# Layer B's attention: one copy per output bank, halves turned by DMA and added by GpSimd, and narrower second-dilation products

## The chip, the cores and the metric

The kernel runs on one core of one Trainium2 chip, as a single program. A time is the device time of one execution in microseconds (us); three executions of the kernel before took 3033.78, 3033.9 and 3038.08 us, median 3033.9. The core has five engines that each run their own list of instructions in order and wait for one another through semaphores: TensorE (PE; its weight loads are shown as PEld), VectorE (DVE), ScalarE (ACT), GpSimd (POOL) and SyncE (SP). SP computes nothing here: it issues DMA transfers, one after the other, and waits before an issue if the transfer's source isn't ready or its target is still in use. TensorE writes to PSUM banks of 128 partitions by 512 float32; DVE and ACT read them.

## The reference

A two-layer decoder trunk on 1024 tokens of width 1024: layer A with native sparse attention and a SwiGLU block, then layer B, whose queries attend over shared keys and values in three head groups of different dilation, and a second SwiGLU block. Only layer B's attention is touched:

```
DILATIONS = ((128, 1), (512, 4), (2048, 16))       # (window, dilation)
def banded_attention(q, k, v, max_dist, dist_scale, rel_bias):
    s = einsum(q, k) * dh ** -0.5                  # per block of 128 queries
    p, denom, m = masked_softmax(s + bias, mask)   # unnormalised exp, its sum, row max
    o = einsum(p, v) / denom
    lse = log(denom) + m
def dilated_attention(h, w_q, k_shared, v_shared, w_out, rel_bias):
    ...                                            # the three (o, lse), merged by softmax over lse
    return o @ w_out
```

There are 16 heads in 4 groups of 4 (g = 0..3), each of 64 columns, and 8 blocks of 128 queries. Dilations 4 and 16 are both handled on tokens ordered by residue modulo 8: a block r of 128 queries of one residue needs 256 keys for dilation 4 and 128 for dilation 16.

## The kernel before, in words

**Precision.** float32 values are used in TensorE as a pair of `float32r` tiles, high and low (`split`, L132: ACT copies the rounded high part, DVE subtracts it). For keys and queries the pair lies in one tile of 128 partitions, high in 64, low in 64.

**Work of a unit.** For each group there are 8 *wide* units (`wide_job`, r = 0..7: dilations 4 and 16 together, 384 columns of scores) and then 8 *near* units (`near_job`, t = 0..7: dilation 1, 128 or 256 columns). Each unit is two jobs, `hp` = 0 and 1, of two heads `e` each. The front of a job (`unit`) makes the score products on PE, adds the bias and takes the row extreme on DVE (L1453), and exponentiates on ACT (L1458). The back, two jobs later (`pipelined(jobs(), 2)`), transposes the probabilities on PE (`transposed`, L275), brings them to SBUF as a pair (`th`, `tl`, L138 and L139), and multiplies by the values into a bank `o` (`mm_pv`, L296 to L298). Banks: 3 for scores (`s`), 3 for transposes (`pt`), 2 for outputs (`o`).

- In a wide unit, one value block is *late*: only the last 64 queries of it count. Its transpose is copied raw, by ACT for hp 0 and DVE for hp 1 (L289), and split by POOL (L290, L291); with `bufs` 5 these share `th` and `tl` with the rest.
- In a near unit, hp 1 isn't split: its transpose is copied raw (L281), by ACT for even t and DVE for odd t, and multiplied as plain float32 (L296).
- The score product of dilation 16 (L1494) is 256 columns wide, of which the last 128 are never read; the last r has 128.

**Evacuation.** Products of values' high and low halves stand in the two partition halves of the bank and are to be added across them. When hp 1 is done, `evac_o` (L302) does this for e = 0, 1: ACT copies the 64 partitions of the other half to SBUF (`ot`, L308), and DVE adds the bank's own half to it (L309), into `o12` (wide) or `oT` (near). `evac_o` is also layer A's.

**Merging and loads.** `merge(g)` weights the two outputs (rows L1524 to L1572), partly among group g's near jobs, partly among group g + 1's wide jobs. Queries, keys, values and bias tables of a group are loaded by SP from HBM into rings of fixed slots: `load` (L1415 queries, L267 and L268 keys, L1419 values), `load_T12` (L1426, L1427) and `load_T0` (L1435, whose tables POOL then masks, L1436). A load waits until the slot's last reader is done. A group's loads are about 13 MB, 11 MB of it in 27 transfers of 256 or 512 KB. SP's transfers use eight semaphores in turn, so transfer n is issued only when transfer n - 8 has landed.

**Order.** The lists of all engines, SP's and POOL's too, are set at build time by a scheduler that plays the program through with its own estimates of time; on the chip each engine runs its list as it stands.

## Time and profile before

The profiled execution spans 3035.7 us on the core (granted clock 0.983 on the mean); the median of the timed executions is 1.8 us below that span.

| stretch of the trace, us | what | length | PE busy | DVE busy | ACT busy | POOL busy | DMA share |
|---|---|---|---|---|---|---|---|
| 0 to 1925 | layer A, its SwiGLU, projections for B | 1925.0 | 1855.8 | 1452.8 | 1004.7 | 1095.5 | 0.35 |
| 1925 to 2245.5 | layer B's attention | 320.5 | 293.82 | 274.28 | 278.60 | 95.50 | 0.60 |
| 2245.5 to 3035.7 | output projection, SwiGLU, final norm | 790.2 | 749.65 | 674.61 | 320.23 | 439.07 | 0.18 |

Busy time is time in which an engine works, by its instructions' spans; spans of neighbouring instructions overlap a little, so an engine can be full below 100%. "DMA share" is the mean busy share of the 16 DMA engines. An instruction's group has a row with its line, engine, operation, names (out<-in), shape, count, then busy us and mean ns of one, then the idle time of the engine before it and what ended that.

### The profile page before, as it was taken

How to read it: one execution, taken by the hardware profiler on the slowest of the kernel's cores; microseconds unless marked ns; L12 is line 12 of the kernel's file. 1: busy time of each engine (PE TensorE's matmuls, PEld its weight loads, DVE VectorE, ACT ScalarE, POOL GpSimd, SP SyncE). 2: the span in 40 equal slices, each digit the busy share in tenths (PEclk: the TensorE clock that was granted, in tenths of full speed). 3: DMA queues.
4: the chain of work that ended last, by engine and by line, in shares of the span. 5: the costliest groups of instructions: out<-in, count | busy, mean ns of one | idle time of the engine just before them, and what ended most of it. 6: DMA issues, size and time to landing. Idle time of an engine off the chain costs nothing.

```text
span 3035.7 us, 44147 instructions
## 1 busy us (share of the span) xinstructions
PE 2899.3 (96%) x14670; PEld 2381.4 (78%) x14670; DVE 2401.7 (79%) x4832; ACT 1603.6 (53%) x3596; POOL 1630.1 (54%) x1751
## 2 busy tenths in 40 slices
PE   7999999999889999999999999899988899999997
PEld 6987888888677877777777778788866787777776
DVE  4432888988988888888876677589899788888887
ACT  5432888887463333333364444689965433333334
POOL 2134666666766555555556787333357755555551
PEclk9999999999999999999999999999999999999999
DMA  6765032121112222222124555876420211112111
GB/s 167 223 191 165 25 103 78 36 56 70 60 53 63 63 67 74 65 59 70 56 95 141 160 160 145 264 209 179 138 94 25 66 55 57 56 46 62 51 45 73
DMA packets 266196, 293.43 MB, mean 97 GB/s; under 512 B 17971, under 2 KB 209347, under 8 KB 265968
## 3 DMA queue, kind: packets, MB, share of 16 engines
q1 hardware_dynamic: 246320, 230.45, 26.3%
q0 software_dynamic: 19648, 60.16, 6.6%
q8 instruction: 116, 1.90, 0.3%
q14 instruction: 112, 0.92, 0.1%
HBM read 227.44 MB, written 78.81 MB: 101 GB/s over the span
## 4 chain that ended last, share of the span: by engine, by line
PE 68%; DVE 16%; ACT 5%; issue 4%; DMA 4%; POOL 2%; SPq 1%; DVEq 0%; ACTq 0%; POOLq 0%
PE ux L165 5%; PE ux L166 5%; PE ux L167 5%; PE uy L166 4%; PE uy L165 4%; PE uy L167 4%; DVE pl L762 4%; PE pt L275 4%; PE dx L166 3%; PE dr L165 3%; PE dx L167 3%; PE dx L165 3%; PE dr L166 3%; PE dr L167 3%; PE mm L165 3%
## 5 line engine op out<-in xcount | busy, mean ns | idle before, releaser
L762 DVE TENSOR_TENSOR pl<-oT,ph 128x512 fp32r<-128x512 f32 x315 | 325.2, 1052 | 41.3 <-ACT ph L761 35.4
L761 ACT ACTIVATE ph<-oT 128x512 fp32r<-128x512 f32 x329 | 199.0, 626 | 228.1 <-PE ux L166 65.8
L275 PE MATMUL pt<-ident,P 128*128 128x128 f32 x1536 | 245.1, 278 | 11.0 <-ACT P L1458 2.7
L761 ACT ACTIVATE ph<-oTb 128x512 fp32r<-128x512 f32 x239 | 143.2, 625 | 189.4 <-PE ux L166 55.7
L762 DVE TENSOR_TENSOR pl<-oTb,ph 128x512 fp32r<-128x512 f32 x229 | 224.4, 1005 | 23.5 <-ACT ph L761 23.4
L820 DVE TENSOR_TENSOR xr<-xr,dr 128x512 f32<-128x512 f32 x336 | 214.6, 679 | 33.9 <-PE dr L167 33.8
L139 DVE TENSOR_TENSOR tl<-pt,th 128x512 fp32r<-128x512 f32 (+1 forms) x320 | 207.1, 651 | 33.8 <-ACT th L138 31.9
L820 DVE TENSOR_TENSOR xr<-xr,dx 128x512 f32<-128x512 f32 x352 | 220.3, 678 | 3.6 <-PE dx L167 2.4
L166 PE MATMUL dx<-pl,ph 128*128 128x512 f32 x512 | 203.4, 401 | 9.7 <-DVE pl L762 9.0
L688 POOL TENSOR_SCALAR P<-P,sm,gates 128x384 f32<-128x384 f32 (+7 forms) x256 | 183.5, 728 | 53.4 <-DVE sm L686 48.0
L275 PEld LDWEIGHTS pt<-ident,P 128*128 128x128 f32 x1536 | 179.8, 142 | 30.0 <-ACT P L1458 6.7
L138 ACT ACTIVATE th<-pt 128x512 fp32r<-128x512 f32 (+1 forms) x320 | 177.2, 563 | 44.3 <-PE pt L275 40.4
L167 PE MATMUL dx<-ph,pl 128*128 128x512 f32 x512 | 200.0, 397 | 0.3 <-DVE pl L762 0.3
L684 ACT ACTIVATE P<-P,m 128x384 f32<-128x384 f32 (+7 forms) x256 | 170.7, 669 | 16.1 <-DVE m L682 8.4
L1081 POOL TENSOR_TENSOR oT<-oT,gffn 128x512 f32<-128x512 f32 x92 | 105.9, 1158 | 136.2 <-DMA oT<-in_ffn_w_up_dram 110.5
L165 PE MATMUL dx<-ph 128*128 128x512 f32 x512 | 157.3, 400 | 6.7 <-DVE xr L820 3.3
L1081 POOL TENSOR_TENSOR oTb<-oTb,gffn 128x512 f32<-128x512 f32 x92 | 106.4, 1165 | 99.1 <-DMA oTb<-in_ffn_w_up_dram 77.0
L298 PE MATMUL o<-tl,V 128*128 128x256 f32 x540 | 148.8, 299 | 7.4 <-POOL tl L291 3.7
L297 PE MATMUL o<-th,V 128*128 128x256 f32 x540 | 151.4, 296 | 2.7 <-ACT th L138 1.4
L290 POOL TENSOR_SCALAR th<-traw 128x128 fp32r<-128x128 f32 (+1 forms) x112 | 75.1, 674 | 129.3 <-ACT traw L289 47.7
L1458 ACT ACTIVATE P<-P,st 128x384 f32<-128x384 f32 (+2 forms) x256 | 139.6, 547 | 7.6 <-PE pt L1569 4.1
L166 PEld LDWEIGHTS dx<-pl,ph 128*128 128x128 f32 x512 | 97.6, 191 | 39.5 <-DVE pl L762 19.4
(617 smaller groups left out, 9582.4 us busy)
## 6 DMA issues: line engine op xcount, KB each, us to landing
qB<-xr POOLq DMA_DIRECT2D x96, 256.0 KB, 4.7
oT<-in_ffn_w_up_dram SPq DMA_DIRECT2D x92, 256.0 KB, 3.0
oTb<-in_ffn_w_up_dram SPq DMA_DIRECT2D x92, 256.0 KB, 3.0
Q<-qB SPq DMA_DIRECT2D x40, 512.0 KB, 7.0
wd<-in_ffn_w_down_dram SPq DMA_DIRECT2D x66, 256.0 KB, 2.6
oT<-in_b_w_q_dram SPq DMA_DIRECT2D x48, 256.0 KB, 3.5
K<-kBs SPq DMA_DIRECT2D x40, 256.0 KB, 9.5
wraw<-in_a_w_in_dram SPq DMA_DIRECT2D x18, 512.0 KB, 4.9
```

Source lines behind the costliest of these rows:

```text
L138: nc.scalar.activation(H_, src, AF.Copy)
L139: nc.vector.tensor_sub(L_, src, f32(H_))
L165: nc.tensor.matmul(ps, lh, rh, start=first, stop=False, skip_group_check=bool(shared))
L166: nc.tensor.matmul(ps, lh, rl, start=False, stop=False, skip_group_check=bool(shared))
L167: return nc.tensor.matmul(ps, ll, rh, start=False, stop=last, skip_group_check=bool(shared))
L275: nc.tensor.transpose(ps[:, i * 128:(i + 1) * 128], b, ident)
L684: nc.scalar.activation(P[:, e, :n], P[:, e, :n], AF.Exp, bias=mm[:, e:e + 1], scale=-1.0, accum_out=sm[:, e:e + 1])
L688: nc.gpsimd.tensor_scalar(P[:, e, :n], P[:, e, :n], sm[:, e:e + 1], gt(g, t, br, 2 * hp + e, 1), op0=OP.mult, op1=OP.mult)
L761: nc.scalar.activation(h, src, AF.Copy)
L762: (eng or nc.vector).tensor_sub(l, src, f32(h))
L820: nc.vector.tensor_add(xs, xs, banks[t])
L1081: nc.gpsimd.tensor_mul(v, v, gains[:, k:k + 4].unsqueeze(2).to_broadcast([128, 4, 128]))
```

## The change

- **Evacuation.** A new `evac_shifted` takes the place of `evac_o` in layer B. The whole bank is copied once to SBUF (`oraw`, two buffers), by ACT for even units and by DVE for odd ones. Then, for each half, SP issues a DMA that moves the other half's 64 partitions by 256 columns (64 KB) across the partitions (`oturn`, two buffers), and POOL adds the two in SBUF. The bank is free after the copy.
- **Second dilation's product.** 128 columns instead of 256, for all r. The first loads of its keys take equal pieces instead of overlapping by 128 columns.
- **Copies.** The late copies and the raw copies of near units are all made by DVE.
- **Buffers.** Late blocks get tiles of their own (`thq`, `tlq`, 128 columns, two buffers); `th` and `tl` have 4 buffers instead of 5; `T0`'s ring has 4 slots instead of 5.

```diff
@@ transposed
-        th = p.tile([128, 512], F32R, name="th", bufs=bufs)
-        tl = p.tile([128, 512], F32R, name="tl", bufs=bufs)
+        z = [128, 128] if q0 else [128, 512]
+        th, tl = [p.tile(z, F32R, name=n + "q" * (q0 > 0), bufs=2 if q0 else bufs) for n in ("th", "tl")]
@@ rings
-        rT0 = Ring("T0", [128, 256], F32, [(bB, 5)])
+        rT0 = Ring("T0", [128, 256], F32, [(bB, 4)])
@@ load_first
-                    ks = slice(2 * lo, 2 * hi) if i == 1 else slice(lo + 128 * (lo > 0), min(hi + 128, S))
+                    ks = slice(2 * lo, 2 * hi) if i == 1 else slice(lo, hi)
@@ before unit
-        unsplit = lambda key, hp: (cp_a, cp_v)[key[2] % 2] if key[1] == 0 and hp == 1 else None
+        def evac_shifted(po, dst, copy):
+
+            ov = po[:].rearrange("p (c e q) -> p e c q", e=2, q=128)
+            raw = wk.tile([128, 2, 2, 128], F32, name="oraw", bufs=2)
+            turn = wk.tile([128, 2, 128], F32, name="oturn", bufs=2)
+            copy(raw, ov)
+            for e in range(2):
+                own, oth = slice(64 * e, 64 * e + 64), slice(64 - 64 * e, 128 - 64 * e)
+                nc.sync.dma_start(turn[own], raw[oth, e])
+                nc.gpsimd.tensor_add(dst[own], raw[own, e], turn[own])
+
+        unsplit = lambda key, hp: cp_v if key[1] == 0 and hp == 1 else None
@@ unit, back
-                th, tl = transposed(wk, of(bs), None, 5, unsplit(key, hp))
+                th, tl = transposed(wk, of(bs), None, 4, unsplit(key, hp))
...
-                    th, tl = transposed(wk, of([late]), (cp_a, cp_v)[hp], 5, q0=64)
+                    th, tl = transposed(wk, of([late]), cp_v, 5, q0=64)
...
-                    evac_o(wk, po, dst)
+                    evac_shifted(po, dst, (cp_a, cp_v)[key[2] % 2])
@@ wide_job, score
-                w = min(256, S - r * 128)
                 with after(prev):
                     for z in range(2):
-                        nc.tensor.matmul(ps[:, 256:256 + w], Q2[hh][:, qs], K2[z][:, r * 128:r * 128 + w],
-                                         start=z == 0, stop=z == 1)
+                        nc.tensor.matmul(ps[:, 256:384], Q2[hh][:, qs], K2[z][:, qs], start=z == 0, stop=z == 1)
```

The scheduler makes new lists from it. Two places matter below.

**SP, where group 0 hands over to group 1** (the loads of group 1's second-dilation tiles: K is its keys, Q its queries, T the bias tables). Before:

```order
L267 DMA K_20381<-kBs 64x1024
L268 DMA K_20381<-kBs 64x1024
L267 DMA K_20382<-kBs 64x1024
L268 DMA K_20382<-kBs 64x1024
L1415 DMA Q_20378<-qB 128x1024
L1415 DMA Q_20379<-qB 128x1024
L1415 DMA Q_20380<-qB 128x1024
L1426 DMA T_20393<-s_76 128x256
L1427 DMA T_20393<-s_77 128x128
L1426 DMA T_20396<-s_76 128x256
L1427 DMA T_20396<-s_77 128x128
```

And now:

```order
L267 DMA K_20399<-kBs 64x1024
L268 DMA K_20399<-kBs 64x1024
L267 DMA K_20400<-kBs 64x1024
L268 DMA K_20400<-kBs 64x1024
L1415 DMA Q_20396<-qB 128x1024
L1415 DMA Q_20397<-qB 128x1024
L1415 DMA Q_20398<-qB 128x1024
L1426 DMA T_20411<-s_76 128x256
L1427 DMA T_20411<-s_77 128x128
L1426 DMA T_20414<-s_76 128x256
L1427 DMA T_20414<-s_77 128x128
L1451 DMA oturn<-oraw 64x256 x4
```

The loads stand as before, but the four turning transfers of group 0's wide units r = 5 and 6 now stand behind them, in the same list. Of the same kind: the four of r = 1 and 2 stand ahead of group 1's first load; then 12 loads come, then the four of r = 3 and 4, then 16 loads (the end of which is shown), then these.

**POOL, where group 1 hands over to group 2** (`th`, `tl` the late blocks' pair, T the first dilation's bias tables). Before:

```order
L290 TENSOR_SCALAR th<-traw 128x128
L291 TENSOR_TENSOR tl<-traw,th 128x128
L1436 AFFINE_SELECT T_22190<-T_22190 128x256
L1436 AFFINE_SELECT T_22195<-T_22195 128x256
L1436 AFFINE_SELECT T_22200<-T_22200 128x256
L1436 AFFINE_SELECT T_23435<-T_23435 128x256
L290 TENSOR_SCALAR th<-traw 128x128
```

And now:

```order
L1452 TENSOR_TENSOR o_20773<-oraw,oturn 64x2x128 x6
L1452 TENSOR_TENSOR oTb<-oraw,oturn 64x2x128 x14
L1436 AFFINE_SELECT T_22251<-T_22251 128x256
L1436 AFFINE_SELECT T_22256<-T_22256 128x256
L1436 AFFINE_SELECT T_22261<-T_22261 128x256
L290 TENSOR_SCALAR thq<-traw 128x128
L1436 AFFINE_SELECT T_22266<-T_22266 128x256
L291 TENSOR_TENSOR tlq<-traw,thq 128x128
L1452 TENSOR_TENSOR oTb<-oraw,oturn 64x2x128 x2
```

POOL had nothing between the last late block of a group and the masking of the tables; now the additions of the last three wide and of seven near units stand there, and the eighth near unit's stand behind the masking.

## The prediction

> **What bounds the kernel now.** I read the spans first, then the busy times by stretch, cut at the first score product of each wide and near stage of layer B's attention (wide, near, of groups 0 to 3 in turn; the columns are PE, PEld, DVE, ACT, POOL, clock, DMA share, GB/s).
>
> ```profile
> core 0: 3035.7 us, clock 0.983
> ...
> 1925.30:1965.20 39.90, 34.65 (x271) 34.00 (x269) 27.79 (x87) 32.24 (x90) 13.21 (x27) 0.91 0.91 275
> 1965.20:1998.00 32.80, 28.04 (x206) 25.50 (x205) 26.06 (x103) 29.05 (x91) 6.75 (x15) 0.95 1.01 275
> 1998.00:2043.50 45.50, 43.90 (x331) 39.86 (x329) 41.53 (x125) 38.96 (x114) 19.12 (x32) 1.00 0.52 153
> 2043.50:2075.40 31.90, 29.50 (x228) 26.53 (x226) 27.76 (x106) 31.25 (x98) 5.01 (x11) 1.00 0.92 252
> 2075.40:2118.80 43.40, 41.73 (x320) 38.14 (x319) 39.90 (x122) 36.88 (x106) 18.18 (x30) 1.00 0.41 129
> 2118.80:2149.10 30.30, 28.04 (x216) 24.76 (x214) 26.52 (x106) 29.67 (x95) 4.65 (x10) 1.00 0.90 249
> 2149.10:2193.90 44.80, 42.86 (x326) 39.28 (x325) 40.38 (x121) 38.08 (x110) 18.29 (x30) 1.00 0.29 85
> 2193.90:2224.50 30.60, 26.10 (x199) 23.03 (x199) 27.92 (x107) 30.04 (x93) 4.58 (x10) 1.00 0.33 124
> ```
>
> A wide stage takes some 44.5 us and is PE's (96% busy) with DVE close behind (91%). A near stage takes some 31 us and is ACT's (98%), DVE at 88%. POOL is idle three quarters of the time. The first two stretches are different: the DMA engines are full, because group 0's and group 1's loads run back to back. In near stages of groups 1 and 2 they are full again (0.92, 0.90) with the next group's loads. So what I ask of the change is what it takes from PE and DVE in wide stages, from ACT and DVE in near ones, and what its transfers meet in SP's queue.
>
> **What it takes from the engines.** Groups by form, over the attention alone:
>
> ```profile
> L308 ACT ACTIVATE ot<-o 64x256 f32<-64x256 f32 x128 | 48.5, 379 | 14.9 <-PE o L296 4.6 <-DVE oTb L309 4.0 <-PE o L298 2.7
> L309 DVE TENSOR_TENSOR oTb<-o,ot 64x256 f32<-64x256 f32 x64 | 26.9, 421 | 8.4 <-ACT ot L308 7.1
> L309 DVE TENSOR_TENSOR o<-o,ot 64x256 f32<-64x256 f32 x64 | 26.9, 420 | 5.8 <-ACT ot L308 4.3
> L281 DVE COPY traw<-pt 128x512 f32<-128x512 f32 x16 | 10.9, 684 | 3.1 <-issue 3.0
> L281 ACT COPY traw<-pt 128x512 f32<-128x512 f32 x12 | 7.0, 581 | 0.2
> L281 ACT COPY traw<-pt 128x256 f32<-128x256 f32 x4 | 1.4, 357 | 0.0
> L289 DVE COPY traw<-pt 128x128 f32<-128x128 f32 x32 | 9.1, 285 | 3.4 <-POOL tl L291 1.1 <-PE pt L275 0.8 <-POOL th L290 0.6
> L289 ACT COPY traw<-pt 128x128 f32<-128x128 f32 x32 | 8.2, 257 | 3.6 <-PE pt L275 3.5
> L1494 PE MATMUL s<-K,Q 128*128 128x256 f32 x224 | 44.9, 285 | 0.0
> L1494 PE MATMUL s<-K,Q 128*128 128x128 f32 x32 | 5.4, 249 | 0.0
> ```
>
> ACT loses 48.5 + 8.2 + 7.0 + 1.4 = 65.1 us and gains 32 whole-bank copies, priced as its own 512-column copy of a bank, 0.581: 18.6. Net -46.5, or -11.6 a group. DVE loses 53.8 and gains 32 copies by 0.684 (21.9), 32 late copies by 0.285 (9.1) and ACT's 16 near copies (12 by 0.684 and 4 of 256 columns by 0.42, between the rows of 128 and 512: 9.9). Net -12.9, or -3.2 a group.
>
> PE: 224 products become half as wide. The rows above give 44.9/224 = 0.200 us and 5.4/32 = 0.169, a saving of 0.031 each. In a stretch where nothing waits, starts lie 0.12 apart at 256 columns and 0.06 after one of 128:
>
> ```profile
> 2111.01 0.28 PE L297 MATMUL o<-th,V 128*128 128x256 f32 x1
> 2111.13 0.28 PE L298 MATMUL o<-tl,V 128*128 128x256 f32 x1
> 2111.25 0.23 PE L297 MATMUL o<-th,V 128*128 128x128 f32 x1
> 2111.31 0.29 PE L275 MATMUL pt<-ident,P 128*128 128x128 f32 x1
> ```
>
> So 224 by 0.031 to 0.06, 7 to 13.4 us, all in wide stages: 1.7 to 3.4 a group.
>
> On the path less counts. In wide stages DVE loses 16 additions (6.7) and gains 4 bank copies (2.7) and 8 late ones (2.3): -1.7; it stands 3 us behind PE. In near stages ACT loses 16 copies of 0.379 and its near copies (2.1) and gains 4 bank copies (2.3): -5.9; DVE, 3.5 behind ACT, loses 6.7 and gains 2.7 and 2.5: -1.5. If the busiest engine alone set each stage, a wide one would shrink by 3.4 and a near one by 3.5 + 1.5 = 5.0, together 8.4 a group and 34 in all. But every job passes through DVE, which works 88 to 91% of both stages, and gives up only 1.5 to 1.7 in each. I take 1.5 for each stage: -3 a group, **-12** in all (bounds 0 and -34). The smaller rings (`T0`, `th`, `tl`) and the first keys' cut I take as nothing: late blocks leave `th` and `tl`, and the first key loads only change their cut.
>
> **What it adds.** POOL gets 128 additions of 64x256. The trace has none with 64 partitions; nearest are POOL's subtraction at 256 columns in layer A and, as upper bound, the strided addition of 512:
>
> ```profile
> L291 POOL TENSOR_TENSOR tl<-traw,th 128x256 fp32r<-128x256 f32 x48 | 35.3, 736 | 0.8
> L1572 POOL TENSOR_TENSOR oTb<-oTb,o 128x512 f32<-128x512 f32 x12 | 19.2, 1618 | 2.6 <-DVE o L1570 2.6
> ```
>
> I take 0.74, the same size: 23.7 us a group on top of POOL's 23, of 75. Hidden.
>
> SP gets 128 transfers of 64 KB. Landing times from issue, in group 0's near stage and, after it, in a quiet stretch of group 2's wide stage:
>
> ```profile
> Q<-qB SPq DMA_DIRECT2D x10, 512.0 KB, 9.5
> K<-kBs SPq DMA_DIRECT2D x9, 256.0 KB, 10.3
> ...
> T<-s SPq DMA_DIRECT2D x4, 128.0 KB, 2.3
> T<-s SPq DMA_DIRECT2D x4, 64.0 KB, 2.1
> ```
>
> and, in a full stretch, SP's issues follow landings (a load can only go when the eighth before it is in):
>
> ```profile
> 2046.52 0.45 SPq L268 DMA_DIRECT2D K<-kBs  x1
> 2047.82 0.33 SPq L1415 DMA_DIRECT2D Q<-qB  x1
> 2049.14 0.44 SPq L267 DMA_DIRECT2D K<-kBs  x1
> 2050.81 0.45 SPq L268 DMA_DIRECT2D K<-kBs  x1
> ```
>
> So a turn takes 2.1 us when the queue is quiet and about 10 when it is full. `oraw` and `oturn` have two buffers, so in a lap of copy (0.7), turn, and two additions (1.5) two units can be evacuated. Quiet: 4.3 us for two, against 9.4 that two units take (75/16 each). Full: 12.2 for two, 6.1 a unit, against 3.9 in a near stage.
>
> First hand-over, group 0 to 1. In SP's new list, turns of units r = 3, 4 stand behind 12 loads and those of r = 5, 6 behind 16 more. At 1.0 to 1.7 us a load (the four rows above) and two buffers plus two `o` banks ahead of the turns, four units can be in flight; the next product with values waits on PE, and everything behind it. A block of 16 loads of mixed size takes some 16 us; in it two units come free, worth 2 x 3.9. So some 8 us are lost behind each of two blocks: +16. From below: if the loads have mostly landed by then, only the turns' own bytes count in a stretch that is full anyway, 32 x 64 KB at 275 GB/s = 7.6. From above, full laps for all 8 near units and 3 wide ones: 11 x 2.2 = 24.
>
> Groups 1 and 2: near stages are full for about two thirds, five units; 5 x 2.2 = 11 as an upper bound each. There the list has only two to four loads between turns, so the queue never fills as before; I take +2 each (0 to 11). Group 3 loads nothing, so 0. At the end the last addition comes a turn and a POOL addition later than ACT and DVE's: 2.1 + 1.5 - 0.8, +3.
>
> Sum: -12 + 16 + 4 + 3 = +11, on 3035.7: 3046.7 in its own profile. The median stood 1.8 below the span: **3045**.
>
> **The rivals.**
>
> *The queue doesn't bind (3025).* Turns land in 2.1 us, if turns and loads interleave on the chip; then only -12 and +3 are left: -9 on 3033.9 is 3025. For it: the attention's DMA share is 0.60 on the mean, and ACT's 98% is real. Against it: landings of 10 us in the stretch where these turns stand. The Trainium skill, page "DMA: Bandwidth & Descriptors", section "Anatomy of one DMA — SWDGE (gpsimd) path", fits a transfer as 2.0 us plus its bytes over 436 GB/s; for a turn an estimate of 2.15 us by that page. The quiet rows agree (2.1), the full ones don't (9.5 to 10.3). Chance 0.19.
>
> *Gain and loss cancel (3034).* The first hand-over costs its lower bound, 7.6, the rest nothing: -12 + 7.6 + 3 = -1. Chance 0.16.
>
> *Every full near stage throttles (3060).* Groups 1 and 2 pay 10 each and group 0 the same 16: -12 + 16 + 20 + 3 = +27. For it: the windows' 0.92 and 0.90. Against it: near loads there may wait, nobody needs them for 20 us. It decides from the third near unit on, at `copy(raw, ov)`, which sits in ACT's and DVE's lists ahead of the next exponentials. Chance 0.2.
>
> *POOL becomes the bound (3080 and more).* At the strided price, 1.6 us, POOL has 23 + 51 = 74 us a group, and its list makes it wait for tables besides:
>
> ```profile
> POOL T L1436 <- DMA T<-sA: 80.5, 6, 24.0
> ```
>
> Some 15 more a group, three times: +45. The strides of the new additions are whole runs of 128, unlike that row's, so 0.03.
>
> *The narrow product doesn't save.* If it costs what 256 columns cost, 6 us come back: inside the range.
>
> **How the numbers follow.** Chances: forecast 0.42, then 0.19, 0.16, 0.2 and 0.03. About 0.2%, 6 us, is what a measurement of this kernel can tell from no change: faster is under 3027.8, slower over 3040.0. The forecast and the two slow rivals are slower: 0.65; cancelling is the same: 0.16; the first rival is faster: 0.19. The range for 8 in 10, from just over the first rival's time to just over the third's: 3026 to 3062; the forecast's own is 3040 to 3053 (first hand-over 11 to 19, gain -15 to -9, ends rounded).
>
> **What would show it.** In the profile after: POOL's L1452 at about 0.74 us; L1451's landing near 2 us in wide stages of groups 1 to 3 and near 10 between 1965 and 2000; ACT's busy time in the attention down by some 46 us, DVE's by some 13; the first score product of group 1 (now at 1998.0) about 13 us later, with long waits on `oturn` at L1452 and on the copies; later groups 72 to 76 us each, as against 73.7 to 77.4. If group 1 starts on time, the forecast is wrong in its main term, and 3026 to 3034 is what is left. If L1452 takes 1.5 us, or groups 1 and 2 take over 80 us each, it is too low.

## The result, and the profile after

The changed kernel takes 3083.9 us (median of 4, 3079.65 to 3089.1), the one before 3036.0 in the same runs: a ratio of 1.0148, 95% interval 1.013 to 1.0167 (the ratio of the two medians, which differs a little, is 1.0158). By the medians that is 48 us slower, against a forecast of 11. Its profiled execution spans 3087.3 us, 51.6 more than that of before.

The windows of the changed kernel, cut as in the prediction (near stage of group 0, then wide and near of groups 1 and 2, wide of group 3; columns PE, PEld, DVE, ACT, POOL, clock, DMA share, GB/s):

```profile
1965.80:1996.50 30.70, 26.09 (x183) 22.16 (x180) 22.39 (x91) 22.79 (x75) 11.74 (x22) 0.94 0.98 278
1996.50:2065.30 68.80, 54.20 (x364) 47.60 (x362) 43.11 (x124) 34.31 (x96) 39.04 (x59) 0.90 0.55 155
2065.30:2103.00 37.70, 29.16 (x222) 26.26 (x220) 26.30 (x100) 25.28 (x82) 13.69 (x23) 1.00 0.92 232
2103.00:2148.50 45.50, 41.96 (x319) 37.68 (x318) 37.64 (x115) 30.74 (x86) 32.66 (x51) 1.00 0.52 149
2148.50:2185.30 36.80, 29.27 (x220) 26.22 (x220) 26.60 (x99) 25.25 (x82) 13.85 (x23) 1.00 0.93 232
2185.30:2232.90 47.60, 43.50 (x320) 40.23 (x319) 37.56 (x115) 30.80 (x86) 32.73 (x51) 0.93 0.37 104
```

In group 1's wide stage and in the near stages no engine is full any more: PE is busy 79% of that wide stage, and 77 to 80% of the near stages of groups 1 and 2, where ACT had been full. In the wide stages of groups 2 and 3 PE is still busy 92 and 91%. The waits of the attention say who stands for whom (engine, tile and line that waits, what it waited for, then us in total, times, longest us):

```profile
POOL o L1452 <- DMA oturn<-oraw: 74.8, 19, 13.0
...
DVE oraw L1448 <- POOL o L1452: 22.2, 9, 7.2
ACT oraw L1448 <- POOL oTb L1452: 22.1, 10, 6.1
PEld o L297 <- DVE oraw L1448: 20.7, 9, 7.3
PE o L297 <- DVE oraw L1448: 19.3, 8, 7.1
```

POOL waits for turns, ACT's and DVE's bank copies for POOL (the buffers of `oraw`), PE for the copies (the `o` bank). One turn of that wheel in the timeline of group 1's start (start, us, engine, line, then the idle time before it and what ended it):

```profile
1996.27 4.26 SPq L1451 DMA_DIRECT2D oturn<-oraw  x4
...
2002.11 3.11 POOL L1452 TENSOR_TENSOR o<-oraw,oturn 64x256 f32<-64x256 f32 x4 [12.99 <-DMA oturn<-oraw]
...
2003.66 0.69 DVE L1448 COPY oraw<-o 128x512 f32<-128x512 f32 x1 [7.17 <-POOL o L1452]
...
2004.40 0.58 PE L297 MATMUL o<-th,V 128*128 128x256 f32 x1 [7.14 <-DVE oraw L1448]
...
2009.40 1.12 SPq L1451 DMA_DIRECT2D oturn<-oraw  x2
...
2017.72 1.51 POOL L1452 TENSOR_TENSOR o<-oraw,oturn 64x256 f32<-64x256 f32 x2 [12.50 <-DMA oturn<-oraw]
...
2020.01 0.58 PE L297 MATMUL o<-th,V 128*128 128x256 f32 x1 [4.89 <-DVE oraw L1448]
```

The bank copied by 2004.35 gets its turn issued at 2009.40, 5 us later, because 13 loads stand between this turn and the one before in SP's list (issued from 2000.63 to 2008.72). It lands 8.2 us after (the chain of waits has `DMA oturn<-oraw` for 8.19 us from 2009.40), and POOL adds at 2017.72. PE stands 7.1 and 4.9 us.

Stage by stage, from the first score product of each stage in the traces (us; "no turn" and "no loads" are experiments below):

| stretch | before | changed | changed, no turn | changed, no loads | before, no loads |
|---|---|---|---|---|---|
| group 0 wide, near | 39.7, 32.9 | 39.6, 30.8 | 42.3, 29.2 | 38.5, 35.4 | 41.2, 29.2 |
| group 1 wide, near | 45.4, 31.9 | **68.7, 37.7** | 48.5, 29.2 | 41.3, 29.0 | 45.4, 31.9 |
| group 2 wide, near | 43.5, 30.2 | 45.6, **36.8** | 42.3, 29.2 | 40.3, 28.9 | 43.5, 30.3 |
| group 3 wide, near with the last merge | 44.8, 48.8 | 47.6, 54.9 | 41.9, 48.0 | 42.5, 51.9 | 44.8, 48.8 |
| after the attention | 793.1 | 799.5 | 792.0 | 797.2 | 791.9 |
| span | 3035.7 | 3087.3 | 3027.0 | 3029.9 | 3030.1 |

### The profile page after: what moved, and what is told of

The parts are those of the page before. It is cut to its first block, busy times and chain, and to the rows that moved or that the text cites. A ratio compares the mean times of both kernels' runs of the same rounds, so it can differ in the third digit from the quotient of the medians.

```text
span 3087.3 us, 44449 instructions
## 1 busy us (share of the span) xinstructions
PE 2908.1 (94%) x14670; PEld 2382.9 (77%) x14670; DVE 2385.1 (77%) x4784; ACT 1557.5 (50%) x3452; POOL 1721.5 (56%) x1879
## 4 chain that ended last, share of the span: by engine, by line
PE 67%; DVE 15%; DMA 7%; issue 4%; ACT 3%; POOL 3%; SPq 1%; DVEq 0%; POOLq 0%; ACTq 0%
PE ux L165 6%; PE ux L166 5%; PE ux L167 5%; PE uy L165 4%; PE uy L166 4%; PE uy L167 4%; DVE pl L762 4%; PE dx L166 3%; PE pt L275 3%; PE dx L165 3%; PE dx L167 3%; PE dr L165 3%; PE dr L166 3%; PE dr L167 3%; DMA oturn<-oraw 3%
## 5 line engine op out<-in xcount | busy, mean ns | idle before, releaser
L688 POOL TENSOR_SCALAR P<-P,sm,gates 128x384 f32<-128x384 f32 (+7 forms) x256 | 183.5, 729 | 53.8 <-DVE sm L686 49.4
L138 ACT ACTIVATE th<-pt 128x512 fp32r<-128x512 f32 (+1 forms) x320 | 176.7, 562 | 59.9 <-PE pt L275 40.5
L297 PE MATMUL o<-th,V 128*128 128x256 f32 x476 | 138.6, 306 | 25.3 <-DVE oraw L1448 19.3
L1469 ACT ACTIVATE P<-P,st 128x384 f32<-128x384 f32 (+2 forms) x256 | 139.4, 547 | 45.6 <-DVE st L1464 40.3
L298 PE MATMUL o<-tl,V 128*128 128x256 f32 x476 | 134.6, 304 | 3.9 <-DVE tl L139 3.0
L166 PE MATMUL dr<-pl,ph 128*128 128x512 f32 x288 | 115.1, 400 | 18.1 <-DVE pl L762 18.0
L1464 DVE CUSTOM_DVE_ANT_0 P<-s,T 128x384 f32<-128x384 f32 (+2 forms) x256 | 114.8, 475 | 17.2 <-PE s L1518 9.3
```

The lines of the kernel that those rows point to most:

```text
L138: nc.scalar.activation(H_, src, AF.Copy)
L166: nc.tensor.matmul(ps, lh, rl, start=False, stop=False, skip_group_check=bool(shared))
L688: nc.gpsimd.tensor_scalar(P[:, e, :n], P[:, e, :n], sm[:, e:e + 1], gt(g, t, br, 2 * hp + e, 1), op0=OP.mult, op1=OP.mult)
```

## Experiments

Ratios are to the kernel before in the same runs, with 95% intervals. The diffs are cut to the lines that matter.

**Which part costs it: four kernels.** Old evacuation put back; no transfers; transfers on two other queues.

```diff
@@ e1
-                    evac_shifted(po, dst, (cp_a, cp_v)[key[2] % 2])
+                    evac_o(wk, po, dst)
@@ e2
-                nc.sync.dma_start(turn[own], raw[oth, e])
-                nc.gpsimd.tensor_add(dst[own], raw[own, e], turn[own])
+                nc.gpsimd.tensor_add(dst[own], raw[own, e], raw[own, 1 - e])
@@ e3, e4
-                nc.sync.dma_start(turn[own], raw[oth, e])
+                nc.gpsimd.dma_start(turn[own], raw[oth, e])      # e3; e4: nc.scalar
```

> The changed kernel with the old evacuation put back (ACT copies the other half, DVE adds the own one); the narrow product, the late and near copies by DVE and the smaller rings stay. Theory (the turns in SP's list cost the 48 us): without turns all of it goes, and what is left is the narrow product's gain against DVE's extra copies, 3025 to 3038 us. Rival 'other edits' (rings of late blocks, 19 us more of DVE): 3055 us or more. Rival 'POOL's additions': the same as the theory, 3025 to 3038.

> The changed kernel without the 128 transfers: POOL adds two halves of the bank copy that lie in the same partitions, so the second term of each sum is not the one that the reference wants; copies, additions and all else stay. Theory (a turn that stands behind loads in SP's list): the bank copies come free after 0.7 + 1.5 us, the first hand-over and the near stages lose nothing, and the gain of 3 us a group is seen, 3015 to 3030 us. Rival 'POOL's additions' (94 us more on POOL, late splits behind them in its list): 3055 us or more. Rival 'other edits': 3055 or more too.

> The changed kernel with the turns issued by POOL, on its own queue, right ahead of the additions that wait for them, so that no turn stands behind a load in SP's list. Theory (SP's list): group 1's wide stage falls from 68.8 us towards 46, near stages of groups 1 and 2 from 37 towards 31, in all 3035 to 3052 us. Rival 'the transfer itself' (2 us or more of latency, two buffers, whatever the queue): 3070 to 3090, with group 1's wide stage still over 60 us. Rival 'POOL's additions': 3080 or more, since POOL's list gets the issues besides.

> The changed kernel with the turns issued by ACT, on its queue, which holds no loads in this stage. Theory (SP's list): as for POOL's queue, 3035 to 3052 us, with ACT some 128 issues busier. Rival 'the transfer itself': 3070 to 3090. An issue by ACT that waits for DVE's copy of the bank holds up the exponentials behind it: if that costs more than SP's list, over 3090.

Measured: e1 3042.6 us, 1.0014 (1.0003 to 1.0024); e2 3029.2, 0.9977 (0.9965 to 0.9989); e3 3112.8, 1.0246 (1.0224 to 1.0269); e4 3096.0, 1.019 (1.0168 to 1.0213). So the transfers, with the waits for them, are the whole loss, and more: without them the change gains 7 us, with POOL's additions all in place. (e1, with the evacuation of before, came out above the theory's 3025 to 3038.) The stages of e2 show it (wide and near of group 1, wide of group 2):

```profile
1996.10:2044.60 48.50, 41.42 (x309) 37.66 (x307) 37.04 (x115) 29.77 (x83) 28.67 (x45) 0.93 0.48 140
2044.60:2073.80 29.20, 28.95 (x236) 27.62 (x236) 27.04 (x101) 25.75 (x84) 17.65 (x28) 1.00 0.94 258
2073.80:2116.10 42.30, 39.97 (x305) 35.85 (x304) 36.76 (x114) 29.69 (x83) 28.61 (x45) 1.00 0.47 136
```

The theory that SP's list alone makes turns late missed: on lists without loads the kernel is slower still, and group 1's near stage begins at 2066.6 (e3) and 2068.6 (e4), no earlier than the changed kernel's 2065.3. In the stretch from 1965 to 2000 a turn takes as long or longer on any queue. The transfers' median time to landing there (last column), first of the changed kernel on SP's queue:

```profile
oturn<-oraw SPq DMA_DIRECT2D x11, 64.0 KB, 4.6
```

of e4 on ACT's:

```profile
oturn<-oraw ACTq DMA_DIRECT2D x9, 64.0 KB, 6.6
```

and of e3 on POOL's:

```profile
oturn<-oraw POOLq DMA_DIRECT2D x10, 64.0 KB, 5.9
```

And the new lists have waits of their own: in e3 POOL stood at a table's mask ahead of the additions (the chain of waits has `DMA T<-sA` for 10.39 us from 2002.77), in e4 the waits ahead of the issues stand in ACT's own list, one of them 5.9 us long.

**What in the transfer costs it.** A third bank copy, in the room of `oturn`, with the transfer landing in the destination itself; transfers that nobody reads; thin transfers; and the narrow product alone.

```diff
@@ e5
-            raw = wk.tile([128, 2, 2, 128], F32, name="oraw", bufs=2)
-            turn = wk.tile([128, 2, 128], F32, name="oturn", bufs=2)
+            raw = wk.tile([128, 2, 2, 128], F32, name="oraw", bufs=3)
...
-                nc.sync.dma_start(turn[own], raw[oth, e])
-                nc.gpsimd.tensor_add(dst[own], raw[own, e], turn[own])
+                nc.sync.dma_start(dst[own], raw[oth, e])
+                nc.gpsimd.tensor_add(dst[own], dst[own], raw[own, e])
@@ e6
-                nc.gpsimd.tensor_add(dst[own], raw[own, e], turn[own])
+                nc.gpsimd.tensor_add(dst[own], raw[own, e], raw[own, 1 - e])
@@ e7
-                nc.sync.dma_start(turn[own], raw[oth, e])
-                nc.gpsimd.tensor_add(dst[own], raw[own, e], turn[own])
+                nc.sync.dma_start(turn[own, :, 0:8], raw[oth, e, :, 0:8])
+                nc.gpsimd.tensor_add(dst[own], raw[own, e], turn[own, :, 0:1].to_broadcast([64, 2, 128]))
@@ e8, in the kernel before
-                w = min(256, S - r * 128)
...
-                        nc.tensor.matmul(ps[:, 256:256 + w], Q2[hh][:, qs], K2[z][:, r * 128:r * 128 + w],
-                                         start=z == 0, stop=z == 1)
+                        nc.tensor.matmul(ps[:, 256:384], Q2[hh][:, qs], K2[z][:, qs], start=z == 0, stop=z == 1)
```

> The changed kernel with the transfer landing in the destination itself, POOL adding the bank copy onto it there; the room of the turn's buffers goes to a third bank copy. Queue, order of issue and bytes stay. Theory A (the lap: a bank copy comes free only after its turn and POOL's addition, and two of them are too few): half or more of the 58 us between the kernel with turns (3087) and the one without (3029) comes back, 3040 to 3058 us. Theory B (POOL stands in its list at an addition that waits for its turn, and the late splits behind it come late): 3072 to 3090, since that wait stays. Theory C (the bytes, or the loads that they push back): 3072 to 3090.

> The changed kernel with all 128 transfers in their place, but nobody reads what they bring: POOL adds two halves of the bank copy that lie in the same partitions (the second term of each sum is not the one that the reference wants). A bank copy is still free only when its transfers have read it. Theory A (the lap of bank copies): the transfer stays in the lap, the addition runs beside it, 3060 to 3085 us. Theory B (POOL's wait): it is gone, 3027 to 3045. Theory C (bytes): 3072 to 3090.

> The changed kernel with turns of 8 of each 128 columns (4 KB instead of 64 KB), and POOL adding one turned column to all 128 (so the sums are not the reference's); every issue, wait, buffer and operation of the same size stays. Theory A and theory B: latency and place in the list stay, 3065 to 3090 us. Theory C (the bytes): 3027 to 3045.

> The kernel before with the second dilation's score product 128 columns wide and nothing else. If PE's 7 to 13 us of a wide stage's path are saved: 3022 to 3030 us. If DVE, close behind PE, takes it all, 3032 to 3038. If the narrow product doesn't save, 3036 to 3042, as with the old evacuation put back into the changed kernel (3042.6).

Measured: e5 3075.1, 1.0122 (1.0098 to 1.0146); e6 3054.8, 1.006 (1.0039 to 1.0082); e7 3066.0, 1.0083 (1.0053 to 1.0113); e8 3043.4, 1.0016 (1.0001 to 1.0031).

No single theory fits. With a third copy group 1's near stage begins 9.7 us earlier (2055.6; 6.2 earlier if each kernel is counted from its own first score product of the attention), and the later stages of the attention gain nothing. Transfers that nobody awaits, but that must have read a copy before it is free, give 29 us back, where theory A allowed up to 24 and theory B 39 or more. The windows of e6, wide and near of groups 1 and 2:

```profile
1993.60:2058.70 65.10, 52.22 (x356) 46.26 (x356) 42.60 (x124) 33.51 (x95) 35.83 (x55) 0.92 0.58 163
2058.70:2094.00 35.30, 31.54 (x241) 28.71 (x240) 28.00 (x105) 26.89 (x86) 17.72 (x29) 1.00 0.92 257
2094.00:2134.10 40.10, 37.93 (x300) 35.02 (x299) 35.86 (x111) 28.75 (x83) 28.34 (x45) 1.00 0.53 155
2134.10:2172.70 38.60, 31.74 (x240) 28.72 (x240) 28.23 (x105) 27.12 (x87) 17.90 (x29) 1.00 0.89 236
```

Beside e2's, group 1's wide stage (65.1) and the near stages (35.3, 38.6) stay long though nobody awaits the turns, so there the lap of copy and transfer is long enough to bind by itself. Group 2's wide stage is as short as without transfers: there the loss comes with the awaiting. Theory C fell too in the main (3066 where it had 3027 to 3045): with a sixteenth of the bytes group 1's near stage begins at 2064.7 as against 2065.3, and a 4 KB turn lands as late as a 64 KB one in the same stretch (e7):

```profile
oturn<-oraw SPq DMA_DIRECT2D x12, 4.0 KB, 4.5
```

From there to the end of the attention e7 gains 8 us on the changed kernel by its trace, 5.8 of them in the last stage (49.1 against 54.9), and 8.4 more behind it; by the medians it is 18 us faster in all. So the bytes are not what makes the first hand-over slow, but later they count. The Trainium skill, page "DMA: Bandwidth & Descriptors", has two rules for this: in "Issuing engines are not separate DMA queues", that transfers of all issuing engines run on the same 16 DMA engines; and in "Queues, rings and completion order", that the write which signals a landing waits for all earlier writes of that DMA engine, across its queues. The landing times fit both (5.9 and 6.6 us on queues without loads, 4.5 us for 4 KB); no run here isolates either rule. The narrow product alone saves nothing (e8).

**Is it the loads?** Both kernels with groups 1 to 3 working on group 0's tiles (e9, e10), and POOL freed of the late splits (e11; e12 with e5's three copies).

```diff
@@ e9 (changed), e10 (before)
             def loads12(g):
-                load(1, g)
-                load_T12(g, 0)
-                load(2, g)
-                load_T12(g, 1)
+                for k in ((1, ), (2, )):
+                    grp[k + (g,)] = grp[k + (0,)]
+                for e in range(2):
+                    grp["T12", g, e] = grp["T12", 0, e]
...
-                        load(0, g)
-                        load_T0(g)
+                        if g == 0:
+                            load(0, g)
+                            load_T0(g)
+                        else:
+                            grp[0, g], grp["T0", g] = grp[0, 0], grp["T0", 0]
@@ e11, e12
-                    th, tl = transposed(wk, of([late]), cp_v, 5, q0=64)
+                    th, tl = transposed(wk, of([late]), None, 5, q0=64)
```

> The changed kernel with groups 1 to 3 of layer B's attention working on group 0's queries, keys, values and tables again, without loads of their own (so three quarters of the attention's output are not the reference's); turns, copies and additions stay. To be read against the kernel before with the same loads left out (the next run). Theory 1 (turns late because loads stand ahead of them in SP's list and on the DMA engines): the changed one is within 5 us of the other or up to 15 faster. Theory B (POOL's wait for a turn of 2 us or more, at every unit, loads or not): 20 to 40 us slower than the other. Both as far as I can tell now: some 20 of the 48 us from the loads, 30 from the wait, so 10 to 30 slower.

> The kernel before with groups 1 to 3 working on group 0's queries, keys, values and tables, without loads of their own (three quarters of the attention's output are not the reference's). Its stages after the first are PE's and ACT's, with DMA idle: 5 to 10 us off the first hand-over, 3024 to 3034 us.

> The changed kernel with the late blocks split by ACT and DVE straight from the bank, so that POOL has no split in its list, only additions (and tables, and the merge): DVE keeps one operation a block of 0.28 us, ACT gets 64 of 0.26 (17 us, of the 44 that it won). Theory B (late splits stand behind an addition that waits for its turn, and PE for them): 3050 to 3062 us, wide stages of groups 2 and 3 from 45.6 and 47.6 towards 42. Theory A (the lap of bank copies and SP's list): 3075 to 3092, since copies wait as before.

> The last edit together with the turn landing in place and three bank copies. If POOL's wait and the lap are the two parts of the loss outside the first hand-over: 3030 to 3048 us. If the two are one and the same wait seen from two sides, no more than the better of the two alone: 3050 to 3075.

Measured: e9 3029.5, 0.9971 (0.9958 to 0.9983); e10 3035.7, 0.9996 (0.9984 to 1.0007); e11 3083.4, 1.0154 (1.0134 to 1.0174); e12 3079.0, 1.0133 (1.0114 to 1.0153). This settles it: with the same turns, waits and additions, but no loads of groups 1 to 3 beside them, the changed kernel is 6 us ahead of its counterpart by the medians, and level by the spans of the profiled executions (3029.9 and 3030.1). The loads cost the kernel before nothing that is told apart (0.9996; I had expected 5 to 10 us), and the changed one 54 us by the medians (3083.9 against 3029.5). My mixed guess (10 to 30 slower) was wrong; theory 1 alone was right, which puts the loss on the loads but doesn't part their place in SP's list from what they do to the DMA engines. Without them a turn lands in 2.0 us in the median:

```profile
oturn<-oraw SPq DMA_DIRECT2D x101, 64.0 KB, 2.0
```

In e9's windows (wide and near of group 1, wide of group 2) PE is full, in the near stage too:

```profile
1998.80:2040.10 41.30, 39.94 (x310) 36.33 (x308) 36.92 (x114) 30.29 (x84) 27.93 (x42) 1.00 0.10 24
2040.10:2069.10 29.00, 29.00 (x238) 27.68 (x236) 26.79 (x104) 26.19 (x85) 17.60 (x28) 1.00 0.17 42
2069.10:2109.40 40.30, 39.27 (x305) 35.62 (x303) 35.72 (x111) 29.66 (x83) 27.46 (x42) 1.00 0.10 24
```

Taking the late splits out from behind POOL's waiting addition gains nothing (e11: 3083.4 against 3083.9), and e12 lies above both of its ranges.

**The order in SP's list, and turns where it is quiet.** e13 hands a group's loads out two or three at a time between jobs; e14 adds e5's third copy; e15 keeps the turn for 27 units alone, and there lets it land in the destination as in e5, with two bank copies; e16 is e15 with the wide product and the first key loads of before.

```diff
@@ e13 (load, load_T12 and load_T0 yield after each transfer)
+            def some(n):
+                for _ in range(n):
+                    next(pending[0], None)
...
                         yield lambda: near_job(g, t, hp)
+                        some(3)
...
-                        loads12(g + 1)
+                        pending[0] = loads12(g + 1)
@@ e15
-            turn = wk.tile([128, 2, 128], F32, name="oturn", bufs=2)
...
-                nc.sync.dma_start(turn[own], raw[oth, e])
-                nc.gpsimd.tensor_add(dst[own], raw[own, e], turn[own])
+                nc.sync.dma_start(dst[own], raw[oth, e])
+                nc.gpsimd.tensor_add(dst[own], dst[own], raw[own, e])
...
-                    evac_shifted(po, dst, (cp_a, cp_v)[key[2] % 2])
+                    g_, w_, r_ = key
+                    if g_ == 0 or (r_ >= 3 if w_ else r_ <= 1):
+                        evac_o(wk, po, dst)
+                    else:
                         evac_shifted(po, dst, (cp_a, cp_v)[key[2] % 2])
```

> The changed kernel with each group's loads issued two or three at a time between the jobs of the stage instead of all at once; in SP's list the runs of 12 and 16 loads ahead of group 0's later turns become runs of 2 to 8, and the list of groups 1 to 3 stays as it was. Theory 'the wait in SP's list sets the first hand-over': turns of group 0 wait 3 to 6 us instead of 5 to 20 there, half of the 21 us by which group 0 ends late comes back, 3070 to 3076 us. Theory 'the DMA engines are full, so a turn is late wherever it stands' (5 to 8 us landings on queues of their own): 3080 to 3090.

> Loads spread as before, with the turn landing in place and three bank copies. If list wait and lap are separate parts: 3060 to 3068 us (10 less than with either alone). If three copies already hide what the spread would save: 3070 to 3078.

> The changed kernel with the turn only for units whose transfer is issued when few loads run (groups 1 to 3, wide units 0 to 2 and near units 2 to 7: 27 of 64 units), and the old evacuation by ACT and DVE for the rest. Theory (a turn costs only among loads, and gains else): 3028 to 3036 us, as against 3042.6 with the old evacuation everywhere. If a turn costs wherever it is: 3050 to 3065, in proportion to the 27 units.

> The last kernel with the second dilation's score product 256 columns wide as before. If the narrow product saves nothing (as alone, 3043 against 3040 of the same runs): within 4 us of the last kernel, 3024 to 3036 us. If it saves the 7 to 13 us of PE once DVE and ACT are relieved: 3038 to 3046.

Measured: e13 3070.1, 1.0121 (1.0106 to 1.0137); e14 3077.4, 1.0145 (1.0119 to 1.0171); e15 3049.2, 1.0056 (1.0035 to 1.0076); e16 3055.6, 1.0075 (1.0053 to 1.0097). With the runs of loads cut, group 1's near stage begins at 2057.0, 8.3 us earlier (6.6 counted from each kernel's own first score product), as the list theory wanted; so the order in SP's list is a part of the first hand-over's loss. That the full DMA engines are the rest is argued from the landing times on queues of their own (e3, e4), not shown by a run. A third copy on top (e14) adds nothing. e15 missed: it is slower than the old evacuation everywhere (1.0056 against e1's 1.0014), not faster. So did e16. Between e15 and e16 the narrow product's part is not told apart (the intervals overlap). In e15 the turns of near units 5 to 7 of groups 1 and 2 met loads all the same and landed in 4.9 to 8.4 us; POOL waited 56.0 us in 13 waits for turns into `oTb`, up to 20.4 (such a wait also holds the time before the issue).

**The turn without a transfer.**

```diff
@@ e17 (e18: with e11's edit)
-                nc.sync.dma_start(turn[own], raw[oth, e])
+                nc.gpsimd.tensor_copy(turn[own], raw[oth, e])
```

> The changed kernel with each turn done by a POOL copy of 64x256 from half to half instead of a transfer. Theory (the loss is the transfer among loads): POOL gets 128 copies of 0.5 to 0.75 us besides its additions, 64 to 96 us, some 75% busy in a group, copy to addition takes 2 us wherever loads run, 3024 to 3040 us. Rival (POOL's list, now with splits, copies and additions, becomes the bound): 3050 to 3090.

> The same with the late blocks split by ACT and DVE, so that POOL loses 63 us of splits and ACT gets 17. If POOL binds in the run before, this one is 10 us or more faster than it, 3024 to 3040 us. If not, the same as it or up to 5 slower (ACT's extra work).

Measured: e17 3063.6, 1.0081 (1.0064 to 1.0098); e18 3039.7, 1.0008 (0.9994 to 1.0022). POOL's copy takes 0.4 us, less than the addition (POOL's groups in e17):

```profile
L1451 POOL COPY oturn<-oraw 64x256 f32<-64x256 f32 x128 | 50.8, 397 | 50.6 <-DVE oraw L1448 41.0 <-ACT oraw L1448 4.2
L1452 POOL TENSOR_TENSOR oTb<-oraw,oturn 64x256 f32<-64x256 f32 x64 | 48.5, 758 | 4.4
```

With the splits in POOL's list it binds, as the rival had it; without them (e18) the kernel is 24 us faster and not told apart from the one before. No version that computes the reference beat the kernel before.

## Why the prediction was wrong

The direction was right, and so was the mechanism (turns late beside loads, bank copies and PE behind them); the size was not. In the sum's own terms, by the table of stages (the turn's cost is changed against no turn, the gain no turn against before; each is one profiled execution):

| term | forecast | measured |
|---|---|---|
| gain of what is removed | -12 (0 to -34) | -8.7 (3027.0 - 3035.7) |
| first hand-over, to the end of group 1's wide stage | +16 (7.6 to 24) | 1.6 (later start) - 2.7 + 1.6 + 20.2 = +20.7 |
| near stages of groups 1 and 2 | +4 (0 to 22) | 8.5 + 7.6 = +16.1 |
| wide stages of groups 2 and 3 | nothing | 3.3 + 5.7 = +9.0 |
| tail | +3 | 6.9 in the last stage + 7.5 behind it = +14.4 |
| sum | +11 | +51.5 |

The two sums are 40.5 us apart: 12.1 in the near stages, 11.4 in the tail, 9.0 in the wide stages of groups 2 and 3, 4.7 in the hand-over, 3.3 in the gain.

**The step that failed** most is "There the list has only two to four loads between turns, so the queue never fills as before; I take +2 each". I had the bound (five units, 2.2 us each) and the windows' 0.92 and 0.90 in hand and took nearly nothing. The list was misread too. Bank copies run some units behind the score products, so the turns issued around group 1's near stage are those of its wide units r = 3 to 7: 4 loads stand ahead of the first of them, then 3, 6, 5 and 8 between one unit and the next, and group 2's list is the same. The turns of r = 3 to 6 in SP's timeline, two to a unit, and the landing times of all turns from 2066 to 2106:

```profile
2063.18 1.25 SPq L1451 DMA_DIRECT2D oturn<-oraw  x2
...
2067.17 2.29 SPq L1451 DMA_DIRECT2D oturn<-oraw  x2
...
2077.62 1.18 SPq L1451 DMA_DIRECT2D oturn<-oraw  x2
...
2085.83 1.12 SPq L1451 DMA_DIRECT2D oturn<-oraw  x2
```

```profile
oturn<-oraw SPq DMA_DIRECT2D x16, 64.0 KB, 3.4
```

The first turns of these four units landed after 7.8, 10.2, 8.6 and 7.1 us, three of the bank copies had stood 1.9 to 6.2 us before their turn was issued, and PE's busy share fell from 92 to 77%. The rival "every full near stage throttles" (+27) had this term right, at 10 each, but not the others: its 3060 is still 24 us short. Its doubt, that near loads may wait since nobody needs them for 20 us, was beside the point: not the loads wait, the turns do.

**Two more steps put at nothing or at the quiet price.** "Group 3 loads nothing, so 0" is not so: each group's first-dilation tiles are loaded in its own wide stage, and the output projection's weights (`ow`, 8 transfers of 512 KB) in group 3's near stage. The prediction's own windows have a DMA share of 0.29 and 0.33 there. In the changed kernel turns landed after up to 4.8 us in both stages, and the wide stages of groups 2 and 3, which the sum leaves out, cost 9.0. The tail took the quiet 2.1 us; its last stage lost 6.9, which goes with the turns: it takes 54.9 here, 49.1 with thin ones (e7), 48.3 with turns that nobody awaits (e6) and 48.0 without any.

**The first hand-over** lies between its forecast and its upper bound by its own mechanism, copies of the bank in pairs behind runs of loads, but that the term came so near is partly luck. I counted 16 us for each of two blocks of loads, less two units; SP issued the 12 loads in 9.1 us (1971.21 to 1980.34) and the 16 in 11.7 (1984.57 to 1996.27). In return two blocks of 13 loads were not counted: group 0's own first-dilation loads ahead of the turns of r = 1 and 2, and the 13 ahead of r = 7's, above. From its end to the issue of its first turn each of the first nine bank copies stood 5.0 to 20.2 us, and their transfers then took 2.0 to 8.2, 4.6 in the median from 1965 to 2000 and not the "near 10" that I named: the wait in the list was the longer part. The 1.6 us of later start lie ahead of the attention's first score product, which comes between 1920.0 and 1930.9 in the runs of this document; they can't be put down to the turns. In the tile's view from 1934 to 1998 the changed kernel made seven bank copies, where without transfers (e2) it made 14 and the kernel before 21 of its half moves, 10.5 units. The changed kernel (ns min/median/max, first and last start):

```profile
L1448 ACT COPY oraw<-o x4: 571/583/587, 1940.6 to 1989.1; 128x512 f32<-128x512 f32 x4
L1448 DVE COPY oraw<-o x3: 691/692/693, 1945.8 to 1987.5; 128x512 f32<-128x512 f32 x3
```

The kernel before, ACT's half moves:

```profile
L308 ACT ACTIVATE ot<-o x21: 376/381/382, 1941.8 to 1995.3; 64x256 f32<-64x256 f32 x21
```

I expected group 1's start to move, and it didn't (1996.5 against 1998.0): PE's list has a first product of group 1 ahead of the stop, so the delay shows inside the wide stage. The sentence "If group 1 starts on time, the forecast is wrong in its main term" was a bad sign to name: the start of a stage is no measure where products run ahead.

**A cost that was not in the sum:** after a stop PE runs at a lower clock. Five stretches from 1996.5 (stop, work, work, stop, work), clock in the column behind POOL:

```profile
1996.50:2004.40 7.90, 0.76 (x6) 0.58 (x4) 0.69 (x1) 1.19 (x6) 2.14 (x3) 0.81 0.88 282
2004.40:2011.20 6.80, 6.80 (x35) 6.00 (x36) 3.31 (x10) 2.19 (x6) 0.75 (x2) 0.71 1.10 333
2011.20:2015.20 4.00, 3.62 (x24) 2.80 (x23) 3.84 (x19) 3.52 (x12) 0.00 (x0) 1.00 1.05 241
2015.20:2020.00 4.80, 0.00 (x0) 0.00 (x0) 0.79 (x3) 0.06 (x1) 1.63 (x3) 0.85 1.04 304
2020.00:2025.80 5.80, 5.72 (x17) 4.57 (x17) 1.23 (x2) 0.59 (x1) 4.65 (x9) 0.54 0.24 61
```

At 0.71 for 6.8 us and 0.54 for 5.8, the two stops cost an estimated 2.0 and 2.7 us on top of themselves (6.8 x 0.29, 5.8 x 0.46). Over the whole stage the clock is 0.90, as against 1.00 before; without turns it is 0.93, so not all of this is the turns'. The Trainium skill, page "TensorE: Matmul & The Clock Gate", section "Part 1: The HAM clock gate", says that the clock halves after an idle window of some 3.4 us and comes back after as much sustained work; the trace agrees in kind (0.54 for 5.8 us behind the stop of 4.8, then 1.00 from 2025.8 to 2036).

**The gain** came out smaller than forecast, within its bounds: -7 by the medians without transfers (-8.7 by the spans), -6 without loads, against -12. It is spread otherwise: without loads groups 1 and 2 gain 11.6 us together (4.1 and 2.9, 3.2 and 1.4), twice my 3 a group, and group 3 nothing in sum (2.3 gained in its wide stage, 3.1 lost in the last). The narrow product's term gives nothing by itself: its price fell (43.4/256 = 0.170 us of busy time after, 0.200 before), the time did not. The old evacuation with the other edits is some 6 us slower than before (e1), so what gain there is comes from the new evacuation without its transfers.

**What I said would show it:** L1452 at 0.73 (as priced), bank copies at 0.58 and 0.69 (as priced), ACT's busy time in the attention down from 277.2 to 232.9 (44; forecast 46), DVE's in the rows that change down by 12.6 (53.8 against 22.0 + 10.0 + 9.2 added; forecast 13), group 1's and 2's lengths 106.4 and 82.4 us, over the 80 that I had named as the sign that the forecast is too low. POOL did not become the bound. The fit of 2.0 us plus bytes over 436 GB/s that I took from the Trainium skill, page "DMA: Bandwidth & Descriptors", is given there for transfers that GpSimd issues, and the turns were SP's; without loads they landed in 2.0 us all the same (e9).

Slips in the working that move nothing: the four rows of SP's issues lie 1.3 to 1.7 us apart, not 1.0 to 1.7; -1 on 3033.9 is 3033, not 3034; and the forecast's own bounds add up to 3037 to 3051, not 3040 to 3053.

What stays open: how the wait for a turn costs group 2's and 3's wide stages 3 to 6 us beside loads but nothing without them, and the share of list wait and full DMA engines in the near stages.

## What to carry to other kernels

A transfer put into a chain between engines is to be priced at its landing time beside the loads that run there (here up to 10.2 us against 2.0), with the time that it stands behind loads in its issuer's list on top (here up to 20.2 us), and at that times the number of units that come by in a full stretch. Neither another queue (5.9 and 6.6 us) nor a sixteenth of the bytes (4.5) brought the landing time back to the quiet one here. Where two buffers and two banks tie such a transfer to PE, its latency sets the pace as soon as both are in use. Take the upper bound where the profile's DMA share stands at 0.9, and look for loads in every stage before a term is put at nothing.

## What was not expected of the hardware

A DVE operation on two SBUF tiles that takes 0.68 us took 11.12 right behind the attention, while POOL ran eight operations on SBUF without a break, and ended half a microsecond behind them. The tile's view of `pl` in the changed kernel:

```profile
L762 DVE TENSOR_TENSOR pl<-ta,ph x1: 11121/11121/11121, 2292.2 to 2292.2; 128x512 fp32r<-128x512 f32 x1
L762 DVE TENSOR_TENSOR pl<-tb,ph x1: 677/677/677, 2303.2 to 2303.2; 128x512 fp32r<-128x512 f32 x1
```

POOL's timeline there, first and last of the eight and the next:

```profile
2292.67 1.26 POOL L828 TENSOR_TENSOR ta<-oTb 128x512 f32<-128x512 f32 x1
...
2301.49 1.26 POOL L831 TENSOR_TENSOR ow<-ow,ow 128x512 f32<-128x512 f32 x1
2303.38 1.64 POOL L835 TENSOR_TENSOR ta<-ta,oTb 128x512 f32<-128x512 f32 x1 [0.63 <-DVE pl L762]
```

PE waited 11.2 us for it. Five other kernels of these runs (e5, e9, e12, e14, e16) show the same operation at 11.10 to 11.13 us. Counted from the last product of the last merge, these six take 792.6 to 800.2 us to the end (median 797.3), and the thirteen whose operation is never that long 788.5 to 796.1 (median 792.0; e3, with one of 6.15 us, is left aside). So some 5 of the 6.4 us that the changed kernel loses behind the attention may be this collision and not the turns; it isn't shown, and e5 has the 11.1 us and loses nothing there (792.6). And a 4 KB transfer took as long as one of 64 KB beside loads (4.5 and 4.6 us), as shown above.
